# All output tiles of the down projections with the weights stationary, and the last tile's end in two spare banks

## The chip, the cores and the metric

One core of one Trainium2 chip runs the whole kernel in one launch. The metric is the device time of one execution in microseconds; the median of three runs is given. Granted clock 1.00 is TensorE at its 2.4 GHz level.

## What is computed

One layer of an encoder: a half-step SwiGLU feed-forward block, token mixing by two kinds of attention, and a second half-step feed-forward block, each behind a modulated RMS norm. 256 tokens, width 2048, hidden width 5632, all in float32. The change touches the third product of the two feed-forward blocks, the down projection, and its residual:

```python
def swiglu(x, w_gate, w_up, w_down):
    return (jax.nn.silu(x @ w_gate) * (x @ w_up)) @ w_down

f = swiglu(modulate(rms_norm(h, g_ffn1[l]), sh1, sc1), w1_gate[l], w1_up[l], w1_down[l])
h = h + 0.5 * gt1[:, None, :] * f
...
f = swiglu(modulate(rms_norm(h, g_ffn2[l]), sh3, sc3), w2_gate[l], w2_up[l], w2_down[l])
h = h + 0.5 * gt3[:, None, :] * f
```

## The kernel before

**Layout.** The residual h is kept with features on partitions: 16 tiles of 128 features x 256 tokens (`h[d]`, d = 0 to 15). The hidden activation is 44 tiles of 128 hidden features (`hid[f]`), each holding a high part and a low part of 256 tokens side by side. Every weight and activation is split into a high and a low part, and a product is made of three terms: high by high, high by low, low by high.

**The stream of weights.** All weights come through one stream of units (class `Flow`). A unit is 128 x 1024, eight blocks of 128 x 128, and is loaded by SyncE's queue (L77), rounded to its high part by ScalarE three units ahead (L84), and its low part is made by VectorE two units ahead (L91). `step()` advances one unit: it issues these conversions, then the functions that were registered for this unit with `at` or `at_abs` (phase 0, 1, 3), and between them, at a rate set by `pace`, side jobs on VectorE that make the modulation vectors from `w_ada` (L197, with their own loads, L211). `next()` hands out one block (128 x 128), `half()` four blocks side by side (128 x 512). The order of all instructions is the order of the program text; no scheduler reorders it.

**The down stage** is `ffn_down`, called once for each feed-forward block (L626 and L917). It has 16 x 44 blocks, so 88 units, and two forms.

- Three groups (`DG = 3`, L479 to L486) of four output tiles each: the activation is stationary and the weights stream. For each f, and each half t of the tokens, `mm3` (L223) issues three matmuls of 512 columns into the bank of that half (L224 high by high, L225 high by low, L226 low by high). The result has tokens on partitions, so `turn` brings it back: ScalarE copies the two banks to SBUF (L464), in the next unit TensorE makes eight 128 x 128 transposes (L472) into two banks (`pr`), and VectorE folds each tile into h, one operation for a tile (`finish`, L448).
- Four single tiles (L487 to L495): the weight block is stationary and the activation streams. `mm2` (L228) issues one matmul of 512 columns, high weight by high and low activation (L229), and one of 256, low weight by high activation, into the first half of the same bank (L230). `finish` folds both halves of the bank into h (L448, two operations for a tile). For the last tile the folds are issued directly after its last matmul (L497).

In the first stage `finish` also makes the squares of the folded tile (ScalarE) and their running sum (VectorE, L287) for the next norm; `stat.finish` multiplies the sum and the last square by a matrix of ones on TensorE (L300, L302) with matmuls between and after that only keep the engine busy (L296). The next stage's first matmul waits for that norm. In the second stage `finish` stores each tile; the last store ends the kernel.

**What stands before it.** The up projection hands over its last group of hidden tiles (40 to 43) inside the down stage: `hid_soon` combines gate and up on VectorE in the second unit (L385), transposes in the third (L394), rounds on ScalarE in the fourth (L400) and makes the low part on VectorE in the fifth (L407).

Of the kernel before, what the change touches and what calls it, by code (L numbers as in the profile page):

```python
# [9 lines left out]
F32 = mybir.dt.float32  # L10
F32R = mybir.dt.float32r
AF = mybir.ActivationFunctionType
ALU = mybir.AluOpType
AX = mybir.AxisListType

P = 128
S = 256
D = 2048
KT = D // P
DFF = 5632  # L20
FT = DFF // P
# [3 lines left out]
NEG = -1e30  # L25
CW = 1024
SPLIT1 = (3, 8, 16)
DG = 3
SPLIT2 = (4, 10, 16)
PLAN = ((4, 6, 9, 11), (8, 10, 13, 15), (12, 14, 17, 19), (16, 18, 21, 23))  # L30
PLAN_L = ((4, 6, 9, 11), (6, 8, 11, 13), (7, 9, 12, 14), (9, 11, 14, 15))
# [119 lines left out]
def build(tc, a):  # L151
    nc = tc.nc
    with ExitStack() as ctx:
        cp = ctx.enter_context(tc.tile_pool(name="cp", bufs=1))
        wp = ctx.enter_context(tc.tile_pool(name="wp", bufs=2))
        sp = ctx.enter_context(tc.tile_pool(name="sp", bufs=2))
        pb = ctx.enter_context(tc.tile_pool(name="pb", bufs=8, space=bass.MemoryType.PSUM))

        def bank(nm):
            return pb.tile([P, 512], F32, tag="b", name=nm)  # L160
# [4 lines left out]
        fl = Flow(tc, a, wp, srcs)  # L165
# [3 lines left out]
        ident = cp.tile([P, P], F32, name="ident")  # L169
# [6 lines left out]
        h = [h4[k // 4][:, k % 4, :] for k in range(KT)]  # L176
# [28 lines left out]
        def mod(j, k):  # L205
            assert (j, k) in modded, (j, k)
            return acc[:, j, k : k + 1]
# [15 lines left out]
        def mm3(out, lh, ll, rh, rl, first, last, **kw):  # L223
            nc.tensor.matmul(out, lh, rh, start=first, stop=False, **kw)  # L224
            nc.tensor.matmul(out, lh, rl, start=False, stop=False, **kw)  # L225
            nc.tensor.matmul(out, ll, rh, start=False, stop=last, **kw)  # L226

        def mm2(ps, lh, ll, r, first, last):  # L228
            nc.tensor.matmul(ps, lh, r.rearrange("p t s -> p (t s)"), start=first, stop=False)  # L229
            nc.tensor.matmul(ps[:, :S], ll, r[:, 0, :], start=False, stop=last)  # L230
# [115 lines left out]
        part, hid = {}, {}  # L346
# [96 lines left out]
        def ffn_down(jg, stat=None, out=None):  # L443
            def finish(d, u, ps):

                def e0():
                    for p_ in ps:
                        nc.vector.scalar_tensor_tensor(h[d], p_, mod(jg, d), h[d], ALU.mult, ALU.add)  # L448

                fl.at_abs(u, e0)  # L450
                if stat is not None:
                    box = []
                    fl.at_abs(u + 1, lambda: box.append(stat.square(h[d])))
                    fl.at_abs(u + 2, lambda: stat.add(box[0]))
                if out is not None:
                    fl.at_abs(u + 1, lambda: nc.sync.dma_start(out[d], h[d]))

            def turn(G, ps):
                box = {}

                def e0():
                    for t in range(2):
                        box[t] = sp.tile([P, 512], F32, tag="th", bufs=2, name="dt")
                        nc.scalar.copy(box[t], ps[t])  # L464

                def e1():
                    for i in range(2):
                        pt = bank("pr").rearrange("p (f s) -> p f s", f=2)
                        for f in range(2):
                            cs = slice((2 * i + f) * P, (2 * i + f + 1) * P)  # L470
                            for t in range(2):
                                nc.tensor.transpose(pt[:, f, t * P : (t + 1) * P], box[t][:, cs], ident)  # L472
                        for f in range(2):
                            finish(4 * G + 2 * i + f, fl.u + 1 + i, [pt[:, f, :]])

                fl.at(0, e0)
                fl.at(1, e1, 3)

            for G in range(DG):  # L479
                ps = [bank("pd") for t in range(2)]  # L480
                for f in range(FT):
                    whi, wlo = fl.half()
                    for t in range(2):
                        ts_ = slice(t * P, (t + 1) * P)
                        mm3(ps[t], hid[f][:, 0, ts_], hid[f][:, 1, ts_], whi, wlo, f == 0, f == FT - 1)
                turn(G, ps)  # L486
            for d in range(4 * DG, KT):  # L487
                ps = bank("pd")
                for f in range(FT):
                    if d == KT - 1 and f == FT // 2:  # L490
                        fl.pace(0.0)
                    w = fl.next()
                    mm2(ps, *w, hid[f], f == 0, f == FT - 1)
                if d < KT - 1:
                    finish(d, fl.u, [ps[:, :S], ps[:, S:]])  # L495
            for p_ in (ps[:, :S], ps[:, S:]):
                nc.vector.scalar_tensor_tensor(h[d], p_, mod(jg, d), h[d], ALU.mult, ALU.add)  # L497
            if stat is not None:
                stat.add(stat.square(h[d], True))
                stat.finish(hid[0])  # L500
            if out is not None:
                nc.sync.dma_start(out[d], h[d])
# [70 lines left out]
        for c in range(KT):  # L573
            nc.tensor.matmul(
                pm[:, 0:1], zero[c // 8][:, c % 8 * P : (c % 8 + 1) * P], sc2[:, c : c + 1],
                start=c == 0, stop=c == KT - 1)
# [345 lines left out]
def _consts():  # L922
    pos = np.arange(S, dtype=np.float32)
    inv = np.power(500000.0, -np.arange(0, 32, 2, dtype=np.float64) / 32).astype(np.float32)
    ang = (pos[:, None] * inv[None, :]).astype(np.float32).astype(np.float64)
    cs, sn = np.cos(ang).astype(np.float32), np.sin(ang).astype(np.float32)
    rope = np.stack([np.concatenate([cs, cs], 1), np.concatenate([-sn, sn], 1)], 1)
    rope = np.ascontiguousarray(rope.reshape(2, P, 2, 32).transpose(1, 0, 2, 3))
    i = np.arange(S)
    df = i[:, None] - i[None, :]  # L930
    cnt = (np.abs(df) <= 64).astype(int) + (df % 4 == 0) + (df % 16 == 0)
    lnc = np.where(cnt > 0, np.log(np.maximum(cnt, 1)), NEG).astype(np.float32)
    col = i % 64
    start = np.clip(col - 8, 0, 48)
    ok = (col[None, :] >= start[:, None]) & (col[None, :] < start[:, None] + 16)
    nam = np.where(ok, 0.0, NEG).astype(np.float32)
    row = i // 64
    idx = (row[None, :] - row[:, None] + 7) * 31 + np.clip(col[None, :] - col[:, None], -15, 15) + 15

    def lay(m):  # L940
        return np.ascontiguousarray(m.reshape(2, P, S).transpose(1, 0, 2))

    return rope, lay(lnc), lay(nam), idx
# [15 lines left out]
def _arrays(inputs):  # L959
    g = {k: np.asarray(v) for k, v in inputs.items()}  # L960
    rope, lnc, nam, idx = _consts()
    c = np.ascontiguousarray

    def vec(v):
        return np.asarray(v).reshape(-1, P).T

    wq = g["w_qkv"][0].reshape(8, 2, P, 3, 4, 512).transpose(4, 3, 0, 2, 1, 5).reshape(4, 3, 8, P, CW)
    arr = {
        "x": c(g["x"][0].T.reshape(4, 4, P, S).transpose(0, 2, 1, 3)),
        "w_ada": c(g["w_ada"][0].reshape(2, CW, 9 * KT, P).transpose(2, 0, 3, 1)),  # L970
        "vecs": c(np.concatenate([
            vec(g["g_ffn1"][0]), vec(g["g_mix"][0]), vec(g["g_ffn2"][0]),
            vec(g["g_out_na"][0]), vec(g["g_out_dil"][0]), vec(g["c"][0]), vec(g["b_ada"][0])], axis=1)),
        "qkg": c(np.stack([g["qn_na"][0], g["kn_na"][0], g["qn_dil"][0], g["kn_dil"][0]])),
        "rope": rope, "lnc": lnc, "nam": nam,
        "nab": c(g["rpb_na"][0].reshape(8, -1)[:, idx].reshape(8, 2, P, S).transpose(0, 2, 1, 3)),
        "w_qkv": c(np.stack([wq[g_, j, k_] for g_, j, k_ in QKV_ORDER])),
        "w_o": c(g["w_o"][0].reshape(2, 8, P, KT, P).transpose(0, 3, 2, 1, 4).reshape(2 * KT, P, CW)),
    }

    def stream(blocks):
        return c(blocks.reshape(-1, 8, P, P).transpose(0, 2, 1, 3).reshape(-1, P, CW))

    def halves(units):
        return c(units.reshape(-1, 2, P, 512).transpose(0, 2, 1, 3).reshape(-1, P, CW))

    arr["w_zero"] = c(g["w_ada"][0][:, :P].reshape(2, 8, P, P).transpose(0, 2, 1, 3).reshape(2, P, CW))
    for l, cuts in ((1, SPLIT1), (2, SPLIT2)):
        gu = np.stack([g[f"w{l}_gate"][0], g[f"w{l}_up"][0]]).reshape(2, KT, P, FT // 4, 512)
        gu = gu.transpose(3, 0, 1, 2, 4)  # L990
        arr[f"w{l}_s"] = halves(gu[:2, :, : cuts[0]].transpose(2, 0, 1, 3, 4))
        arr[f"w{l}_a"] = halves(gu[2:, :, : cuts[0]])
        arr[f"w{l}_b"] = halves(gu[:, :, cuts[0] : cuts[1]])
        arr[f"w{l}_c"] = halves(gu[:, :, cuts[1] :])
        wd = g[f"w{l}_down"][0]
        arr[f"w{l}_d"] = np.concatenate([
            halves(wd[:, : 512 * DG].reshape(FT, P, DG, 512).transpose(2, 0, 1, 3)),
            stream(wd[:, 512 * DG :].reshape(FT, P, KT - 4 * DG, P).transpose(2, 0, 1, 3))])
    return arr


# [20 lines left out]
```

## Time and profile before

| | us |
|---|---|
| median of three runs | 1912.9 (1912.8 to 1914.55) |
| the profiled execution, its own time | 1914.67 |
| its span, first to last instruction | 1912.9 |
| TensorE matmul busy | 1896.2 |
| VectorE busy | 1526.6 |
| ScalarE busy | 895.5 |
| first down stage, first to last matmul start | 519.4 to 763.4 |
| second down stage, first to last matmul start | 1664.8 to 1908.9 |

The rows further down come from this profiled execution. Times on the left of a row are microseconds from the start of the span. PE is TensorE's matmul side and PEld its loading of stationary operands; DVE is VectorE, ACT is ScalarE, SP is SyncE. A matmul's duration in a row reaches over the start of the next, since they are pipelined; the distance of two starts is what one costs in a stream.

### The profile page before, as it was taken

The page shows a single profiled execution, that of the slowest core. Times are in us where ns is not written, and L with a number is a line of the kernel's source. Part 1 is how long each engine was busy: PE and PEld are TensorE (multiplying, and loading weights), DVE is VectorE, ACT ScalarE, POOL GpSimd, SP SyncE. Part 2 cuts the span into 40 slices and gives each one's busy share as a digit, 9 for nine tenths or more (in the row PEclk, how much of TensorE's full clock was granted, in tenths as well). Part 3 has the DMA queues.
Part 4 walks back from the last instruction along what each step waited for, and adds up shares of the span by engine and source line. Part 5 has one row for each costly group of instructions (what it writes and reads, how often), then busy time and mean ns, then how long its engine had stood idle before and what let it go on. Part 6 is the DMA issues. An engine that isn't in the chain of part 4 may idle for free.

```text
span 1912.9 us, 25124 instructions
## 1 busy us (share of the span) xinstructions
PE 1896.2 (99%) x9105; PEld 1591.3 (83%) x9105; DVE 1526.6 (80%) x2086; ACT 895.5 (47%) x1226; POOL 1.2 (0%) x7
## 2 busy tenths in 40 slices
PE   8999999999999999999999999999999999999999
PEld 6888888888888888888888998888888888888888
DVE  7989988888889888778887988777777888876444
ACT  5654444444444443555555544654443544443342
POOL 0000000000000000000000000000000000000000
PEclk9999999999999999999999999999999999999999
DMA  8998987777799999576766656998888767687664
GB/s 327 368 337 310 308 291 243 247 260 251 245 361 360 350 359 363 186 244 217 243 207 201 209 186 214 310 306 276 271 275 264 220 213 227 220 286 255 200 198 131
DMA packets 140813, 503.85 MB, mean 263 GB/s; under 512 B 15632, under 2 KB 17936, under 8 KB 140688
## 3 DMA queue, kind: packets, MB, share of 16 engines
q1 hardware_dynamic: 140688, 502.25, 78.0%
q8 instruction: 71, 1.16, 0.2%
q14 instruction: 54, 0.44, 0.1%
HBM read 500.09 MB, written 2.10 MB: 263 GB/s over the span
## 4 chain that ended last, share of the span: by engine, by line
PE 94%; DVE 4%; issue 1%; ACT 0%; POOL 0%; POOLq 0%; DVEq 0%
PE pu L224 16%; PE pu L226 16%; PE pu L225 16%; PE pd L225 6%; PE pd L226 6%; PE pd L224 6%; PE pd L229 4%; PE pd L230 2%; PE pqv L224 2%; PE pqk L224 2%; PE pqq L224 2%; PE pqk L225 2%; PE pqk L226 2%; PE pqq L225 2%; PE pqv L226 2%; PE pqq L226 2%
## 5 line engine op out<-in xcount | busy, mean ns | idle before, releaser
L84 ACT CAST hiw<-rw 128x1024 fp32r<-128x1024 f32 x656 | 692.2, 1055 | 954.4 <-PE pu L226 446.1
L91 DVE TENSOR_TENSOR low<-rw,hiw 128x1024 fp32r<-128x1024 f32 x656 | 802.0, 1223 | 336.3 <-issue 126.7
L224 PE MATMUL pu<-hiw,nx 128*128 128x512 f32 x1352 | 527.7, 390 | 0.0
L226 PE MATMUL pu<-hiw,nx 128*128 128x512 f32 x1352 | 526.1, 389 | 0.0
L225 PE MATMUL pu<-low,nx 128*128 128x512 f32 x1352 | 526.1, 389 | 0.0
L226 PEld LDWEIGHTS pu<-hiw,nx 128*128 128x128 f32 x1352 | 253.8, 188 | 53.0
L225 PEld LDWEIGHTS pu<-low,nx 128*128 128x128 f32 x1352 | 253.9, 188 | 51.9
L224 PEld LDWEIGHTS pu<-hiw,nx 128*128 128x128 f32 x1352 | 253.9, 188 | 51.8
L224 PE MATMUL pd<-hiw,hd 128*128 128x512 f32 x528 | 205.9, 390 | 0.0
L226 PE MATMUL pd<-hiw,hd 128*128 128x512 f32 x528 | 205.4, 389 | 0.0
L225 PE MATMUL pd<-low,hd 128*128 128x512 f32 x528 | 205.4, 389 | 0.0
L197 DVE CUSTOM_DVE_ANT_0 ra<-ra,cb,acc 128x1024 f32<-128x1024 f32 x143 | 185.7, 1299 | 0.2
L229 PE MATMUL pd<-hd,hiw 128*128 128x512 f32 x352 | 122.5, 392 | 0.0
L226 PEld LDWEIGHTS pd<-hiw,hd 128*128 128x128 f32 x528 | 99.1, 188 | 20.6
L224 PEld LDWEIGHTS pd<-hiw,hd 128*128 128x128 f32 x528 | 99.1, 188 | 20.4
L225 PEld LDWEIGHTS pd<-low,hd 128*128 128x128 f32 x528 | 99.1, 188 | 20.3
L362 DVE TENSOR_TENSOR pt<-pt,pu 128x512 f32<-128x512 f32 x176 | 112.4, 680 | 0.0
L230 PE MATMUL pd<-hd,low 128*128 128x256 f32 x352 | 98.6, 280 | 0.0
L197 DVE CUSTOM_DVE_ANT_0 ra<-ra,cb,vec 128x1024 f32<-128x1024 f32 x63 | 80.5, 1279 | 0.0
L229 PEld LDWEIGHTS pd<-hd,hiw 128*128 128x128 f32 x352 | 65.8, 187 | 14.4
L224 PE MATMUL pso<-ox,hiw 128*128 128x256 f32 x256 | 73.9, 289 | 0.0
L225 PE MATMUL pso<-ox,hiw 128*128 128x256 f32 x256 | 73.1, 286 | 0.0
(154 smaller groups left out, 2000.5 us busy)
## 6 DMA issues: line engine op xcount, KB each, us to landing
ra<-in_w_ada_dram SPq DMA_DIRECT2D x286, 512.0 KB, 4.9
rw<-in_w_d_dram SPq DMA_DIRECT2D x176, 512.0 KB, 4.6
rw<-in_w_c_dram SPq DMA_DIRECT2D x154, 512.0 KB, 4.3
rw<-in_w_b_dram SPq DMA_DIRECT2D x121, 512.0 KB, 4.8
rw<-in_w_qkv_dram SPq DMA_DIRECT2D x96, 512.0 KB, 4.2
rw<-in_w_a_dram SPq DMA_DIRECT2D x63, 512.0 KB, 4.9
rw<-in_w_o_dram SPq DMA_DIRECT2D x32, 512.0 KB, 3.6
rw<-in_w_s_dram SPq DMA_DIRECT2D x14, 512.0 KB, 4.5
```

Source lines behind the costliest of these rows:

```text
L84: self.nc.scalar.copy(t, self.raw[self.nhi])
L91: self.nc.vector.tensor_tensor(t, self.raw.pop(self.nlo), self.hi[self.nlo].bitcast(F32), ALU.subtract)
L197: nc.vector.tensor_tensor_reduce(out=raw, in0=raw, in1=cb[:, b * CW : (b + 1) * CW], scale=scale, scalar=init, op0=ALU.mult, op1=ALU.add, ...
L224: nc.tensor.matmul(out, lh, rh, start=first, stop=False, **kw)
L225: nc.tensor.matmul(out, lh, rl, start=False, stop=False, **kw)
L226: nc.tensor.matmul(out, ll, rh, start=False, stop=last, **kw)
L229: nc.tensor.matmul(ps, lh, r.rearrange("p t s -> p (t s)"), start=first, stop=False)
L230: nc.tensor.matmul(ps[:, :S], ll, r[:, 0, :], start=False, stop=last)
L362: nc.vector.tensor_tensor(part[G][:, j, t, :], part[G][:, j, t, :], ps[t], ALU.add)
```

## The change

The three groups and their `turn` are gone: all sixteen output tiles take the form with the weight block stationary, in the order d = 0 to 15, and each is folded by `finish` with two operations, in the unit that follows its last block. The array of the down weights is laid out for that, as `stream` blocks throughout; it has as many units as before.

The last tile is cut: its first 36 hidden tiles go to its bank `ps` as the others do, and the last eight blocks (one unit) go to two other banks. First come eight matmuls of 256 columns, high weight by low activation, into `pl`; then the two folds of `ps` and the fold of `pl` are issued; then sixteen matmuls of 256 columns, high and low weight by high activation, into `ph`, and the fold of `ph` follows the last of them.

```diff
-DG = 3
...
-            def turn(G, ps):
...
-            for G in range(DG):
-                ps = [bank("pd") for t in range(2)]
-                for f in range(FT):
-                    whi, wlo = fl.half()
-                    for t in range(2):
-                        ts_ = slice(t * P, (t + 1) * P)
-                        mm3(ps[t], hid[f][:, 0, ts_], hid[f][:, 1, ts_], whi, wlo, f == 0, f == FT - 1)
-                turn(G, ps)
-            for d in range(4 * DG, KT):
+            def fold(d, p_):
+                nc.vector.scalar_tensor_tensor(h[d], p_, mod(jg, d), h[d], ALU.mult, ALU.add)
+
+            for d in range(KT):
                 ps = bank("pd")
-                for f in range(FT):
+                body = FT if d < KT - 1 else FT - 8
+                for f in range(body):
                     if d == KT - 1 and f == FT // 2:
                         fl.pace(0.0)
                     w = fl.next()
-                    mm2(ps, *w, hid[f], f == 0, f == FT - 1)
+                    mm2(ps, *w, hid[f], f == 0, f == body - 1)
                 if d < KT - 1:
                     finish(d, fl.u, [ps[:, :S], ps[:, S:]])
+            ws = [fl.next() for f in range(8)]
             for p_ in (ps[:, :S], ps[:, S:]):
-                nc.vector.scalar_tensor_tensor(h[d], p_, mod(jg, d), h[d], ALU.mult, ALU.add)
+                fl.at(0, lambda p_=p_: fold(d, p_))
+            pl_, ph_ = bank("pl")[:, :S], bank("ph")[:, :S]
+            for f in range(8):
+                nc.tensor.matmul(pl_, ws[f][0], hid[body + f][:, 1, :], start=f == 0, stop=f == 7)
+            fl.run(0)
+            fold(d, pl_)
+            for f in range(8):
+                r = hid[body + f][:, 0, :]
+                nc.tensor.matmul(ph_, ws[f][0], r, start=f == 0, stop=False)
+                nc.tensor.matmul(ph_, ws[f][1], r, start=False, stop=f == 7)
+            fold(d, ph_)
...
         wd = g[f"w{l}_down"][0]
-        arr[f"w{l}_d"] = np.concatenate([
-            halves(wd[:, : 512 * DG].reshape(FT, P, DG, 512).transpose(2, 0, 1, 3)),
-            stream(wd[:, 512 * DG :].reshape(FT, P, KT - 4 * DG, P).transpose(2, 0, 1, 3))])
+        arr[f"w{l}_d"] = stream(wd.reshape(FT, P, KT, P).transpose(2, 0, 1, 3))
```

## Rows read from the trace of the kernel before

**Rows 1.** The page: span, and busy time, share and instructions of each engine.
```profile
span 1912.9 us, 25124 instructions
PE 1896.2 (99%) x9105; PEld 1591.3 (83%) x9105; DVE 1526.6 (80%) x2086; ACT 895.5 (47%) x1226; POOL 1.2 (0%) x7
```

**Rows 2.** The chain that ended last: shares; then start us, us, engine, line.
```profile
PE 94%; DVE 4%; issue 1%; ACT 0%; POOL 0%; POOLq 0%; DVEq 0%
...
1909.18 0.49 DVE h L497
1909.70 0.48 DVE h L497
```

**Rows 3.** Stretches of the down stages: length, busy us by engine, PEclk, DMA share.
```profile
core 0: us, PE busy (x) PEld busy (x) DVE busy (x) ACT busy (x) POOL busy (x), PEclk, DMA share, GB/s
519.37:580.10 60.73, 60.73 (x273) 50.38 (x272) 54.12 (x66) 25.47 (x25) 0.00 (x0) 1.00 0.96 350
...
701.57:763.50 61.93, 61.93 (x361) 54.67 (x360) 54.40 (x75) 26.59 (x31) 0.00 (x0) 1.00 0.96 351
1664.70:1725.30 60.60, 60.60 (x273) 50.30 (x272) 44.22 (x52) 24.19 (x24) 0.00 (x0) 1.00 0.85 283
...
1847.05:1909.20 62.15, 62.09 (x361) 54.55 (x359) 28.75 (x31) 21.02 (x21) 0.00 (x0) 1.00 0.52 158
```

**Rows 4.** Timeline of PE, second stage, wide groups: start us, us, line, tiles.
```profile
1728.31 1.03 PE L472 MATMUL pr<-ident,dt 128*128 128x128 f32 x8
...
1789.04 1.03 PE L472 MATMUL pr<-ident,dt 128*128 128x128 f32 x8
1789.83 0.48 PE L224 MATMUL pd<-hiw,hd 128*128 128x512 f32 x1
1790.14 0.40 PE L225 MATMUL pd<-low,hd 128*128 128x512 f32 x1
1790.38 0.39 PE L226 MATMUL pd<-hiw,hd 128*128 128x512 f32 x1
...
1846.82 0.39 PE L226 MATMUL pd<-hiw,hd 128*128 128x512 f32 x1
```

**Rows 5.** Timeline of PE, second stage, the four narrow tiles.
```profile
1847.05 0.39 PE L229 MATMUL pd<-hd,hiw 128*128 128x512 f32 x1
...
1849.86 1.03 PE L472 MATMUL pr<-ident,dt 128*128 128x128 f32 x8
...
1856.28 0.39 PE L229 MATMUL pd<-hd,hiw 128*128 128x512 f32 x1
...
1908.63 0.39 PE L229 MATMUL pd<-hd,hiw 128*128 128x512 f32 x1
```

**Rows 6.** Timeline of PE in the output projection, 256 columns alone.
```profile
1130.97 0.28 PE L224 MATMUL pso<-ox,hiw 128*128 128x256 f32 x1
...
1162.65 0.28 PE L224 MATMUL pso<-ox,hiw 128*128 128x256 f32 x1
```

**Rows 7.** Timeline at the end of the first down stage; idle time and releaser in brackets.
```profile
763.71 1.01 DVE L497 SCALAR_TENSOR_TENSOR h<-pd,acc,h 128x256 f32<-128x256 f32 x2 [1.49 <-PE pd L230]
...
765.23 0.30 PEld L302 LDWEIGHTS pstat<-sq,ones 128*128 128x128 f32 x2 [0.64 <-DVE sq L273]
```

**Rows 8.** Groups of VectorE in 701.57 to 761: count, busy us, mean ns, idle before.
```profile
L287 DVE TENSOR_TENSOR sqa<-sqa,sq 128x256 f32<-128x256 f32 x7 | 2.9, 419 | 0.2
L448 DVE SCALAR_TENSOR_TENSOR h<-pd,acc,h 128x256 f32<-128x256 f32 x6 | 2.9, 481 | 0.1
L448 DVE SCALAR_TENSOR_TENSOR h<-pr,acc,h 128x256 f32<-128x256 f32 x4 | 1.7, 473 | 0.0
```

**Rows 9.** Timeline at the start of the first down stage: the last hidden group.
```profile
524.82 1.04 PE L394 MATMUL ph<-ident,pt 128*128 128x128 f32 x8
...
531.18 1.23 DVE L91 TENSOR_TENSOR low<-rw,hiw 128x1024 fp32r<-128x1024 f32 x1 [0.23 <-issue]
532.32 1.28 DVE L407 TENSOR_TENSOR hd<-ph,hd 128x512 fp32r<-128x512 f32 x2
533.52 1.33 DVE L197 CUSTOM_DVE_ANT_0 ra<-ra,cb,gin 128x1024 f32<-128x1024 f32 x1
```

More of the change, by code (lines that the diff above doesn't have):

```diff
@@ L456, in finish @@
                     fl.at_abs(u + 1, lambda: nc.sync.dma_start(out[d], h[d]))
-            def turn(G, ps):
-                box = {}
-                def e0():
-                    for t in range(2):
[L463 to L477, printed above, removed]
-            for G in range(DG):
-                ps = [bank("pd") for t in range(2)]
-                for f in range(FT):
-                    whi, wlo = fl.half()
-                    for t in range(2):
-                        ts_ = slice(t * P, (t + 1) * P)
-                        mm3(ps[t], hid[f][:, 0, ts_], hid[f][:, 1, ts_], whi, wlo, f == 0, f == FT - 1)
-                turn(G, ps)
-            for d in range(4 * DG, KT):
+            def fold(d, p_):
+                nc.vector.scalar_tensor_tensor(h[d], p_, mod(jg, d), h[d], ALU.mult, ALU.add)
+            for d in range(KT):
                 ps = bank("pd")
-                for f in range(FT):
+                body = FT if d < KT - 1 else FT - 8
+                for f in range(body):
                     if d == KT - 1 and f == FT // 2:
```

## The prediction

> **What bounds the kernel now.** I read the share of busy time first: TensorE is busy for 1896.2 us of a span of 1912.9 us, no other engine for more than 80% [rows 1]. A busy matmul row overlaps the next one, so that share alone proves nothing; the chain that ended last does, since 94% of it is PE and 4% VectorE [rows 2]. So I went to the two down stages and asked whether TensorE ever waits there. Cut into eight stretches (three wide groups and the four narrow tiles of each stage; four of them are shown, the others read alike), PE is busy throughout, but for the last 0.06 us, and the granted clock is 1.00, the 2.4 GHz level [rows 3]. What sets the time there is therefore the start-to-start step of one matmul to the next, plus whatever stands in TensorE's own program order, and nothing that the other engines do. The steps come from the timeline, by dividing the distance of two starts by the matmuls between them; the durations of the rows (0.39 us) are longer than the steps and aren't used.
>
> Two forms of the same product already run side by side in the kernel, which makes this change unusually easy to price. In the wide form (first three groups, four output tiles each) the activation is stationary and the weights stream, 512 columns in each of six matmuls for one hidden tile f. From 1790.38 to 1846.82 there are 249 steps in 56.44 us, 226.67 ns each [rows 4]. In the narrow form (last four output tiles) the weights are stationary, with one 512- and one 256-column matmul for a block. From 1856.28 to 1908.63 there are 151 blocks in 52.35 us, 346.67 ns each [rows 5].
>
> **The change, part by part (one down stage; there are two).**
>
> *The step.* The wide form spends 6 x 512 columns on four output tiles, so for one tile and one f it is 1.5 matmuls: 1.5 x 226.67 = 340.00 ns. The narrow form streams the same 768 columns, but in two matmuls: 346.67 ns, 6.67 ns more. 12 output tiles x 44 f = 528 blocks move from one form to the other: 528 x 6.67 ns = **+3.52 us**. All of it is on the path.
>
> The rows say why. Matmuls of 256 columns alone (the output projection) step at exactly 120.0 ns: 264 of them from 1130.97 to 1162.65 [rows 6]. So 512 columns cost 226.67 and 256 cost 120.0, which sum to the narrow block's 346.67; 256 columns more cost 106.67, and each matmul carries 13.33 ns that don't depend on its width. The change trades 1.5 of these for 2. The Trainium skill, page "TensorE: Matmul & The Clock Gate", section "Back-to-back issue gap", gives a fixed part of only 2.5 ns on a warm clock. The rows contradict it here by a factor of five; with 2.5 ns the step would cost 0.66 us instead of 3.52 us a stage (an estimate from that page), and no other term of mine hangs on it.
>
> *The turn.* After each wide group the result stands with tokens on partitions: ScalarE copies two banks out, TensorE makes eight 128x128 transposes, VectorE folds four tiles into h. The transposes stand in TensorE's order. From one turn's first transpose to the next it is 1789.04 - 1728.31 = 60.73 us [rows 4]; 264 wide matmuls take 59.84; the turn costs 0.89 us (0.79 of transposes, and the 0.31 us step of the first matmul after them, where 0.23 is usual [rows 4]). Three turns: **-2.67 us**. The two ScalarE copies aren't on the path and bring nothing.
>
> *The first blocks in the new form.* The eight narrow blocks right after the switch take 2.81 us (1847.05 to 1849.86), where eight settled ones take 2.77; after the turn's transposes the pace settles [rows 5]. In the changed kernel the switch lies at the start of the stage, and the next transposes (those of the last hidden group) come two units later, so about 16 blocks run at that pace instead of eight: +0.04 us.
>
> *The tail.* Now both halves of the last tile are folded after the last matmul: two VectorE operations starting 0.52 us apart (1909.18 and 1909.70 [rows 2]), and then the store, or in the first stage the square for the statistics; the same pair takes 1.01 us there [rows 7]. In the changed kernel the last eight blocks go into two other banks: 8 matmuls of 256 columns, then 16. The tile's first 36 blocks are folded under these, the low part under the 16, and one fold is left after the last matmul: -0.52 us. It is gained whole: in the second stage only the store follows; in the first the second half of the statistics' product waits for the square, 0.64 us on the loading side [rows 7]. The price is 24 matmuls of 256 columns for eight blocks, 24 x 120.0 = 2.88 us against 8 x 346.67 = 2.77: +0.11 us. The folds under them need 1.3 us of VectorE, where 2.88 us lie open.
>
> *VectorE's extra folds.* Twelve tiles now have two folds instead of one, and the last has four instead of two: 14 x 0.44 us, off TensorE's path as long as VectorE keeps up. The cover is the proof that already runs: in the stretch of the first stage's narrow tiles VectorE had all its usual work, ten folds and seven sums, 54.4 of 61.9 us busy, and PE didn't wait [rows 3, 8]; the changed stage has eight folds and four sums in as long. The low parts of the weights are made two units ahead, about 5.5 us, and the largest backlog that I find (split of the hidden group, then a fold, in one unit each of 3.3 to 3.7 us against a unit of 2.77) is about 1.1 us.
>
> *The last hidden group.* Hidden tiles 40 to 43 are used in the first group's 21st unit now, and in the sixth after the change. Their transposes run at 524.82, and their last split ends on VectorE by 533.52, in the fifth unit [rows 9]. With the longer units of the changed kernel the fifth begins at 531.4 and the sixth at 534.2; the two splits, 0.64 us each behind a low part of 1.14, then end at 533.2 and 533.9, and their first readers come at 534.2 and 534.9. About 1 us is to spare, so 0; if the split came one unit late it would be up to 1.8 us a stage.
>
> *The rest.* As many units, loads and conversions, in the same order, at the same pace of side jobs; the stores of h start earlier and are spread. The gates for the first tiles are long computed. Nothing of it is priced.
>
> **Sum.** 3.52 - 2.67 + 0.04 - 0.52 + 0.11 = +0.48 us a stage, +1.0 us in all. The profiled execution's span goes from 1912.9 to 1913.9 us, and its own time, 1914.67, to 1915.6; the median of the runs shown is 1912.9, 1.8 below the profiled execution's time, so the forecast for the median is **1913.9 us**. A measurement of this kernel can tell about 0.2%, 3.8 us, from no change.
>
> **The rivals.**
>
> *The unsettled pace stays (slower).* The 351.3 ns of the first eight narrow blocks ended with a turn's transposes; the changed kernel has no turns. If only such a break settles the pace, and those of the hidden group don't, the 688 further blocks of a stage cost 4.6 ns more each: 3.2 us, in all 6.4 + 1.0 = +7.4, **1920.3 us**. It decides the sign from about 300 blocks a stage on. For it: the slow blocks are slow one by one, up to the transposes. Against it: the same eight transposes stand in the third unit of the changed stage, and once settled the pace held for 151 blocks without a break.
>
> *A late split or a VectorE backlog (slightly slower).* The tight place is the sixth unit. A split that is a unit late costs 1.8 us a stage: +4.6, **1917.5 us**. Against it: 1 us to spare and VectorE idle before each low part.
>
> *No fixed part (faster).* If a 256-column matmul cost half a 512-column one, both forms would take 340.0 ns a block. The step would cost nothing: -2.67 + 0.04 - 0.52 = -3.15 a stage, -6.3, **1906.6 us**. Two long runs of rows speak against it [rows 5, 6]. The page named above comes nearest to it: by its 2.5 ns, -4.9 us and 1908.0, an estimate.
>
> *The tail brings nothing.* If the last fold doesn't end earlier (VectorE still at the others), the result is +2.0, 1914.9 us: no change either.
>
> **How the numbers follow.** Forecast and idle tail together 0.86, unsettled pace 0.07, late split 0.04, no fixed part 0.03. Within 0.2%: 0.86; slower: 0.11; faster: 0.03. The terms themselves are known to some tenths; the range adds what medians of three differ by (1.7 us between the runs shown) on both sides and most of the late split above: 1912.0 to 1917.0 us.
>
> **What would show it.** Right: narrow blocks stepping at 346.67 ns through the whole stage; a down stage from its first matmul to its last about 1.0 us longer (3.52 - 2.67 + 0.04 + 0.11), PE without a wait; no transposes besides the hidden group's; one fold after the last matmul, ending 0.5 us nearer to it. Wrong: blocks at 350 ns and more after the first 16; a gap of PE before f = 40 of the first tile; VectorE's low parts arriving late; the last fold waiting for VectorE and not for PE.

## The result, and the profile after

The changed kernel takes 1919.84 us (median of ten runs, 1914.59 to 1926.62) against 1914.46 us for the kernel before (ten runs, 1912.64 to 1915.01): a ratio of 1.0034, 95% interval 1.0025 to 1.0043. The forecast was 1913.9 us and no change within 0.2%. It is slower, by 5.4 us, and its runs spread over 12 us where those of before spread over 2.4. The spread is the first clue: whatever was added isn't the same in every execution.

The profiled execution is one of the quick ones, 1916.61 us, with a span of 1914.8 us. In the two down stages it shows the forecast to 0.05 us, which makes it a trap for a reader who looks at one profile only. The page:

```profile
span 1914.8 us, 26084 instructions
PE 1898.3 (99%) x9601; PEld 1612.8 (84%) x9601; DVE 1538.4 (80%) x2114; ACT 889.5 (46%) x1214; POOL 1.2 (0%) x7
```

It answers to [rows 1]: 496 more matmuls, 2 us more of TensorE, VectorE's share as before. The two down stages, cut from the first matmul of the stage to the first matmul behind it (first stage) or to the end of the last fold (second stage), are the view that carries this case. First the kernel before, then the changed one (columns as in [rows 3]):

```profile
519.37:769.38 250.01, 249.34 (x1198) 209.49 (x1196) 219.60 (x289) 104.45 (x115) 0.00 (x0) 1.00 0.95 351
...
1664.84:1910.18 245.34, 244.30 (x1177) 205.74 (x1175) 137.99 (x147) 93.59 (x93) 0.00 (x0) 1.00 0.69 218
```

```profile
519.72:770.26 250.54, 250.06 (x1446) 220.22 (x1445) 224.97 (x303) 101.21 (x109) 0.00 (x0) 1.00 0.95 350
...
1666.06:1911.87 245.81, 245.29 (x1425) 216.45 (x1423) 144.70 (x161) 90.72 (x87) 0.00 (x0) 1.00 0.67 218
```

The stages are 0.53 and 0.47 us longer; the sum in the prediction was 0.48 for each. The rest of the span's 1.9 us is outside them: in the profiles of this study the first down stage begins between 517.4 and 519.7 us and the stretch between the stages takes from 893.8 to 897.5 us, whatever was changed. So times of single executions differ by some microseconds from this alone, and the stages are compared by their own lengths. The narrow blocks, in the timeline of PE of the same execution: first block of tile 1 and of tile 15, 616 blocks apart, in the first and in the second stage.

```profile
535.96 0.39 PE L228 MATMUL pd<-hd,hiw 128*128 128x512 f32 x1
...
749.51 0.39 PE L228 MATMUL pd<-hd,hiw 128*128 128x512 f32 x1
...
1682.30 0.39 PE L228 MATMUL pd<-hd,hiw 128*128 128x512 f32 x1
...
1895.84 0.39 PE L228 MATMUL pd<-hd,hiw 128*128 128x512 f32 x1
```

213.55 us for 616 blocks, 346.67 ns each, in both stages: the pace of [rows 5]. The end of the second stage, VectorE:

```profile
1908.53 1.00 DVE L458 SCALAR_TENSOR_TENSOR h<-pd,acc,h 128x256 f32<-128x256 f32 x2 [4.27 <-PE pd L229]
1909.63 0.48 DVE L458 SCALAR_TENSOR_TENSOR h<-pl,acc,h 128x256 f32<-128x256 f32 x1
1911.39 0.48 DVE L458 SCALAR_TENSOR_TENSOR h<-ph,acc,h 128x256 f32<-128x256 f32 x1 [1.27 <-PE ph L481]
```

Three of the four folds run under the 24 last matmuls, which start from 1908.32 to 1911.07 us, and one is left behind them, where [rows 2] had two. So the page of this execution has no 5 us. They had to be sought in another execution.

### The profile page after: what moved, and what is told of

It reads as the page before. It is cut to its first block, busy times and chain, and to the rows that moved or that the text cites. A ratio compares the mean times of both kernels' runs of the same rounds, so it can differ in the third digit from the quotient of the medians.

```text
span 1914.8 us, 26084 instructions
## 1 busy us (share of the span) xinstructions
PE 1898.3 (99%) x9601; PEld 1612.8 (84%) x9601; DVE 1538.4 (80%) x2114; ACT 889.5 (46%) x1214; POOL 1.2 (0%) x7
## 4 chain that ended last, share of the span: by engine, by line
PE 93%; DVE 6%; issue 1%; ACT 0%; POOL 0%; POOLq 0%; DVEq 0%
PE pd L228 17%; PE pu L223 16%; PE pu L225 16%; PE pu L224 16%; PE pd L229 9%; DVE low L90 2%; PE pqv L223 2%; PE pqk L223 2%; PE pqq L223 2%; PE pqk L224 2%; PE pqk L225 2%; PE pqq L224 2%; PE pqv L225 2%; PE pqq L225 2%; PE pqv L224 2%; PE ph L393 1%
## 5 line engine op out<-in xcount | busy, mean ns | idle before, releaser
L228 PE MATMUL pd<-hd,hiw 128*128 128x512 f32 x1392 | 483.1, 391 | 0.0
L229 PE MATMUL pd<-hd,low 128*128 128x256 f32 x1392 | 389.8, 280 | 0.0
L228 PEld LDWEIGHTS pd<-hd,hiw 128*128 128x128 f32 x1392 | 260.3, 187 | 57.2
L229 PEld LDWEIGHTS pd<-hd,low 128*128 128x128 f32 x1392 | 263.1, 189 | 0.1
L225 PE MATMUL pso<-ox,low 128*128 128x256 f32 x256 | 73.0, 285 | 0.0
L196 DVE CUSTOM_DVE_ANT_0 ra<-ra,cb,gin 128x1024 f32<-128x1024 f32 x48 | 64.2, 1338 | 0.0
L223 PE MATMUL pqk<-hiw,nx 128*128 128x512 f32 x128 | 51.2, 400 | 0.0
L223 PE MATMUL pqv<-hiw,nx 128*128 128x512 f32 x128 | 50.5, 395 | 0.5 <-ACT nx L317 0.5
L223 PE MATMUL pqq<-hiw,nx 128*128 128x512 f32 x128 | 50.9, 398 | 0.0
```

The lines of the kernel that those rows point to most:

```text
L196: nc.vector.tensor_tensor_reduce(out=raw, in0=raw, in1=cb[:, b * CW : (b + 1) * CW], scale=scale, scalar=init, op0=ALU.mult, op1=ALU.add, ...
```

## The experiments

Two words first. **Short pace** and **long pace** are the two steps of a narrow block (one 512- and one 256-column matmul) that the profiles of this order of matmuls show, 346.67 and 353.33 ns on average. Times against before compare medians with those of the kernel before, run beside it on the same chip. The expectations call the short pace fast and the long one slow. The code is abridged: `...` and the comments stand for what isn't shown.

**e1, the changed kernel again**, for a second profile. No edit.

> The changed kernel once more, for the spread of its executions and for another profile. The forecast's theory (one step of 346.67 ns a block, nothing else) gives a span of 1913.9 us in every execution; the ten timed ones had spans from 1912.8 to 1924.8, so something comes on top that varies from one execution to the next. Unsettled pace: some executions keep 351 ns a block over long stretches, up to 6.4 us more, and the profile of a slow one has blocks at 350 ns and over after the first 16. Supply: in some executions TensorE waits, for a weight part, a load or its own instructions, and the profile of a slow one has gaps of 0.5 us and more in a down stage.

Measured: 1921.84 us (1921.75 to 1923.77) against 1912.72, ratio 1.0049 (1.0036 to 1.0063). The profile has a span of 1921.8 us; the stages first, then the first blocks of tile 1 and tile 15 in each stage, as above.

```profile
519.26:774.32 255.06, 254.58 (x1446) 220.84 (x1444) 225.96 (x303) 101.07 (x109) 0.00 (x0) 1.00 0.93 343
...
1668.54:1918.88 250.34, 249.82 (x1425) 217.07 (x1423) 144.65 (x161) 90.41 (x87) 0.00 (x0) 1.00 0.63 213
```

```profile
535.67 0.40 PE L228 MATMUL pd<-hd,hiw 128*128 128x512 f32 x1
...
753.32 0.40 PE L228 MATMUL pd<-hd,hiw 128*128 128x512 f32 x1
...
1684.95 0.40 PE L228 MATMUL pd<-hd,hiw 128*128 128x512 f32 x1
...
1902.60 0.40 PE L228 MATMUL pd<-hd,hiw 128*128 128x512 f32 x1
```

217.65 us for the same 616 blocks: 353.33 ns each, without a wait of PE inside (its busy time fills the stages but for the same 0.5 us as above, the norm behind the first and the last fold of the second), at a granted clock of 1.00. The long pace holds from the transposes of the last hidden group to the end of the stage, 680 blocks x 6.67 ns = 4.53 us, and the stages are 4.52 and 4.53 us longer than in the first profile. The two stages together are 9.05 us longer, the span 7.0: outside the stages this execution was 2.0 us shorter than the first (894.22 us between them against 895.80), so the long pace is the whole excess. The supply theory falls: nothing waited.

Three blocks of this profile show where the time goes, and one block of the first profile (its last row begins the next block):

```profile
599.62 0.40 PE L228 MATMUL pd<-hd,hiw 128*128 128x512 f32 x1
599.85 0.28 PE L229 MATMUL pd<-hd,low 128*128 128x256 f32 x1
599.97 0.40 PE L228 MATMUL pd<-hd,hiw 128*128 128x512 f32 x1
600.21 0.28 PE L229 MATMUL pd<-hd,low 128*128 128x256 f32 x1
600.33 0.40 PE L228 MATMUL pd<-hd,hiw 128*128 128x512 f32 x1
600.56 0.28 PE L229 MATMUL pd<-hd,low 128*128 128x256 f32 x1
600.68 0.40 PE L228 MATMUL pd<-hd,hiw 128*128 128x512 f32 x1
```

```profile
599.75 0.39 PE L228 MATMUL pd<-hd,hiw 128*128 128x512 f32 x1
599.98 0.28 PE L229 MATMUL pd<-hd,low 128*128 128x256 f32 x1
600.09 0.39 PE L228 MATMUL pd<-hd,hiw 128*128 128x512 f32 x1
```

At the long pace the blocks aren't alike: they take 350, 361 and 349 ns in turn, 1.06 us for three. Over the stages of these two profiles the mean step from a 512-column matmul to the 256-column one behind it is 236.67 ns at the long pace and 230.00 at the short, and the step back is 116.67 in both: all the 6.67 ns come behind the matmul of 512 columns.

**e2 and e3, one stage changed.** The three wide groups stay in the other stage.

```diff
-DG = 3
+DGS = (0, 3)          # e3: (3, 0)
+TAIL = (True, False)  # e3: (False, True): the cut tail
...
```

> Only the first down stage is changed (all narrow, cut tail); the second is as before. Forecast's sum: +0.5 us over before. Supply theory: the first stage loads at 0.96 of the DMA engines and VectorE is 90% busy there, so nearly the whole excess of the changed kernel (some +5 us) and its spread are here. Unsettled pace: half of the excess, about +2.5 to +3.2 us, since both stages have the same matmuls.

> Only the second down stage is changed; the first is as before. Forecast's sum: +0.5 us over before. Supply theory: within 1 us of before, since the second stage loads at 0.5 to 0.86 of the DMA engines and VectorE is 46 to 73% busy. Unsettled pace: half of the excess, +2.5 to +3.2 us.

Measured: 1918.45 us for e2 (ratio 1.0034, 1.0021 to 1.0046) and 1920.02 us for e3 (1.0038, 1.0025 to 1.0050) against 1912.72. In their profiles the changed stage has the long pace and the unchanged one doesn't: 255.07 and 245.34 us for the stages of e2, 250.00 and 250.34 for those of e3, so each stage brings its 5.0 us by itself. e3's median is 2 us above that, but its profile isn't: its span is 4.96 us longer than that of the profile before, all of it in the second stage, and outside the stages the two agree to 0.1 us (895.44 us between the stages against 895.46). The 2 us are what that execution of before (1914.67 us) itself lies above the median here. The load on the DMA engines (0.95 in the first stage, 0.67 in the second) makes no difference.

**e4, the tail alone.** Three wide groups in both stages, and only the last tile's end cut.

```diff
-DG = 3
+DGS = (3, 3)
+TAIL = (True, True)
...
```

> The kernel before with the cut tail in both stages and nothing else (three wide groups each). Forecast's terms: -0.52 + 0.11 = -0.41 us a stage, -0.8 us in all. If the tail brings nothing or starves something, 0 or more.

Measured: 1911.79 us (1910.65 to 1914.47, eleven runs) against 1912.72, ratio 0.9997 (0.9988 to 1.0005): not to be told from no change by its time. The stages of its profile tell it:

```profile
519.05:768.68 249.63, 249.17 (x1206) 209.94 (x1204) 220.37 (x291) 104.43 (x115) 0.00 (x0) 1.00 0.95 351
...
1662.52:1907.43 244.91, 244.39 (x1185) 206.18 (x1183) 138.84 (x149) 93.62 (x93) 0.00 (x0) 1.00 0.67 218
```

0.38 and 0.43 us shorter than before, where 0.41 was forecast for each. It is the one part of the change that was run by itself and shortened a stage.

**e5, breaks.** Ahead of tiles 1 to 14 in both stages, a short piece of TensorE work into a spare bank, six kinds in turn.

```diff
...
+                if kind in "AB":   # 8 transposes, 1 transpose
+                    nc.tensor.transpose(idle[:, ...], ident, ident)
+                else:              # 2 x 512, 1 x 256, 3 x 256, 4 x 128 columns
+                    nc.tensor.matmul(idle[:, :w_], hid[0][:, 0, :P], r_, start=True, stop=True)
```

> The changed kernel with a short foreign piece of TensorE work ahead of each output tile d = 1 to 14, in both stages: eight transposes, one transpose, two matmuls of 512 columns, one of 256, three of 256 or four of 128 columns, in turn (their results are not used). Theory that the pace is drawn anew at each break of the alternation and kept until the next: within one execution some tiles step at 346.67 and some at 353.33 ns, and it changes only at a break. Rival, that the pace belongs to the execution (or the chip): all tiles of an execution have one pace, whatever stands between them. Second rival, that only transposes (or a pause) settle it: the tiles behind the transposes differ from those behind plain matmuls.

Measured: 1930.8 us (one run, the breaks' own time included). Each tile behind a break has one pace throughout (twelve blocks at a time, without the first six, take 346.6 to 346.7 or 353.2 to 353.3 ns a block), and it is always one of the two:

| ahead of the tile | tiles at the short pace |
|---|---|
| two matmuls of 512 columns | 4 of 4 |
| one of 256 | 5 of 5 |
| three of 256 | 4 of 5 |
| eight transposes | 2 of 5 |
| one transpose | 2 of 5 |
| four of 128 | 0 of 4 |

So the pace belongs neither to the execution nor to the chip: both occur within one stage, and it changes at breaks alone. Nor does it belong to a place in the weights, since the same tiles had the one pace in the first profile and the other in e1. The table doesn't say what pace stood ahead of a break. By the same trace, the four tiles ahead of the breaks of four 128-column matmuls were short and those behind them long; one transpose left the pace as it was in five of five; four of the five single matmuls of 256 columns stood behind a tile that was short already, and one ended a long one. (The next expectations speak of four tiles behind one matmul of 256 columns; there were five.)

**e6, grouped, and e7, pairs.** The same matmuls in another order: four of 512 columns and then four of 256 for four blocks (e6); high, low, low, high for two blocks (e7).

```diff
-                    mm2(ps, *w, hid[f], f == 0, f == body - 1)
...
+                    for f in fs: nc.tensor.matmul(ps, w[f - f0][0], ...)          # 512 columns
+                    for f in fs: nc.tensor.matmul(ps[:, :S], w[f - f0][1], ...)   # 256 columns
```

> The changed kernel with the same matmuls in another order: of four blocks the four of 512 columns first, then the four of 256. If the extra 6.67 ns of a block comes from alternating 512 and 256 columns matmul by matmul, runs of one width have none of it: 4 x 226.67 + 4 x 120.0 = 1386.7 ns for four blocks, 346.67 each, in every execution, or with one such loss for four blocks at most 348.3; the kernel is at the forecast, +1.0 us over before (at most +3.4), with as little spread as before. If the loss belongs to the stationary weights as such: +8 us as the changed kernel.

> The changed kernel with the order high, low, low, high over two blocks: half as many changes from 512 to 256 columns. If the loss is one for each change of width in this alternation, the slow pace is 350.0 ns a block (half of 6.67), about +1 to +5.7 us over before; if the loss needs the strict alternation, +1.0 us; if it belongs to the stationary weights as such, +8 us as the changed kernel.

Measured against 1913.09: e6 1921.46 us (1919.88 to 1922.22), ratio 1.0039 (1.0026 to 1.0052); e7 1916.71 us (1915.01 to 1920.13), ratio 1.0017 (1.0008 to 1.0026). The grouped order, which I took for the cure, isn't one:

```profile
599.73 1.09 PE L469 MATMUL pd<-hd,hiw 128*128 128x512 f32 x4
600.66 0.64 PE L472 MATMUL pd<-hd,low 128*128 128x256 f32 x4
601.14 1.09 PE L469 MATMUL pd<-hd,hiw 128*128 128x512 f32 x4
602.07 0.63 PE L472 MATMUL pd<-hd,low 128*128 128x256 f32 x4
602.54 1.09 PE L469 MATMUL pd<-hd,hiw 128*128 128x512 f32 x4
```

Eight blocks in 2.81 us are 351 ns each. Four matmuls of 512 columns take 0.93 us to the next start, where 4 x 226.67 are 0.91, while those of 256 take 0.47 to 0.48: the loss sits in the matmuls of 512 columns. It isn't at the change of width: from 530 to 755 us of this profile the step from one of 512 to the next is 233.6 ns on average, and from the last of them to the first of 256 it is 228.3. The profile of e7, its quickest execution, steps at 348.3 ns a block. Fewer changes of width don't give the sum of the single steps back, so the loss isn't simply one for each change.

**e8, the cut tail with the grouped order in the four narrow tiles**, three wide groups kept. The edits of e4 and e6 together.

> The kernel before (three wide groups a stage) with the cut tail and the grouped order in its four narrow tiles. Sum: -0.8 us from the tail; the grouped order takes away the slow pace in the narrow tiles where they have it (at most 176 x 6.67 ns = 1.2 us a stage), and otherwise nothing: -0.8 to -3 us against before.

Measured: 1914.99 us (1913.20 to 1915.65) against 1913.09, ratio 1.0004 (0.9995 to 1.0013): the grouped order gives away what the tail brings. The stages of its profile are 0.3 and 0.2 us longer than before, where the tail alone made them 0.4 shorter.

**e9, e10, e11, one break in each stage**, ahead of tile 1; and **e12**, the changed kernel beside them.

```diff
+                if d == 1:
...
+                    for i in range(n):   # e9: 1 x 256 columns, e10: 2 x 512, e11: 4 x 128
+                        nc.tensor.matmul(idle, hid[0][:, 0, :P], r_, start=True, stop=True)
```

> The changed kernel with one more matmul of 256 columns, into a spare bank, ahead of the second output tile of each down stage; nothing else. In the run with breaks all tiles behind such a matmul stepped at 346.67 ns (four of four). Theory that the break sets the pace for all that follows: tiles 1 to 15 step at 346.67 ns in both stages and in every execution; forecast's +1.0 us, 0.25 for the two matmuls and up to 0.4 for a slow first tile: +1.2 to +1.7 us over before, with no execution more than 3 us above the median. Rival, that the pace of the executions is set by something else (the chip, the loads): a spread as wide as that of the changed kernel beside it.

> The same with two matmuls of 512 columns in place of the one of 256 (four of four tiles at 346.67 ns in the run with breaks). Same theory: +1.7 to +2.4 us over before (two times 0.45 us for the matmuls), and no wide spread. Rival: a spread as wide as that of the changed kernel.

> The same with four matmuls of 128 columns (four of four tiles at 353.33 ns in the run with breaks). Theory: tiles 1 to 15 step at 353.33 ns in both stages and in every execution: 652 blocks x 6.67 ns = 4.35 us a stage, with the forecast's 1.0 and some 0.5 for the matmuls +10 us over before, though it issues about as much work as the other two. Rival: no difference from them.

> The changed kernel beside them on the same chip. Theory: each stage is fast or slow as its only break, the transposes of the last hidden group, leaves it, so executions lie near +1, +5.7 or +10.4 us over before (and within 2.4 us of these, which before spreads by itself), and its profile has one pace, 346.67 or 353.33 ns, from the 17th block on in each stage.

Measured against 1912.86:

| | median, range (us) | ratio, 95% interval | pace from tile 1 on in the profile, first and second stage |
|---|---|---|---|
| e9, one of 256 | 1915.28 (1914.61 to 1917.13, 11 runs) | 1.0011 (1.0002 to 1.0019) | short, short |
| e10, two of 512 | 1918.21 (1918.17 to 1925.86, 6 runs) | 1.0036 (1.0023 to 1.0049) | long, long |
| e11, four of 128 | 1921.32 (1915.73 to 1921.99, 5 runs) | 1.0032 (1.0020 to 1.0044) | short, short |
| e12, changed kernel | 1920.39 (1917.26 to 1921.94, 5 runs) | 1.0035 (1.0022 to 1.0048) | long, short |

e9 first. The blocks of its first tile have the long pace; then comes one more matmul, and the 652 blocks behind it step at 346.67 ns (533.95 to 759.64, 651 steps):

```profile
533.71 0.28 PE L229 MATMUL pd<-hd,low 128*128 128x256 f32 x1
533.83 0.28 PE L467 MATMUL idle<-hd 128*128 128x256 f32 x1
533.95 0.40 PE L228 MATMUL pd<-hd,hiw 128*128 128x512 f32 x1
...
759.64 0.39 PE L228 MATMUL pd<-hd,hiw 128*128 128x512 f32 x1
```

All its eleven runs lie within 2.5 us, where those of before spread over 3.4 beside them, so it isn't likely that any has the 4.5 us of a stage at the long pace. The median is 2.4 us above before, 0.7 more than expected; the stages of the profile are 0.8 longer each. Two matmuls of 0.12 us whose results nobody uses take back two thirds of what the change loses on this chip, by the medians (7.5 us in e12). e10 and e11 came out against their expectations: the kinds that had been 4 of 4 and 0 of 4 in one execution were long, long and short, short in these profiles, and their runs spread like those of the changed kernel. So these kinds don't set the pace. Whether they draw it is less clear: in both stages of e11 the tile ahead of the break was long, and in e5 it was short, so four matmuls of 128 columns changed the pace in six of six cases. A break that turns the pace over would fit these profiles as well as a draw; no run was made to tell the two apart. For two of 512 columns it doesn't hold: behind a long tile they left the pace short three times in e5 and long twice in e10.

e12 has one stage of each, 5.06 and 0.47 us longer than before:

```profile
519.05:774.12 255.07, 254.59 (x1446) 220.74 (x1445) 225.89 (x303) 101.04 (x109) 0.00 (x0) 1.00 0.94 344
...
1669.81:1915.62 245.81, 245.29 (x1425) 216.45 (x1423) 144.68 (x161) 90.75 (x87) 0.00 (x0) 1.00 0.66 217
```

**e13 and e14, the same matmul elsewhere.** e13: ahead of the first and of the 17th block of each stage; e14: ahead of each of the tiles 1 to 14.

```diff
+                    if d == 0 and f in (0, 16):      # e13;  e14: if 0 < d < KT - 1, ahead of the tile
+                        nc.tensor.matmul(bank("idle")[:, :S], hid[0][:, 0, :P], hid[0][:, 0, :], start=True, stop=True)
```

> The changed kernel with one matmul of 256 columns ahead of the first block of each down stage and one ahead of the 17th (right behind the last hidden group's transposes). If one such matmul sets the fast pace wherever it stands: all 704 blocks of both stages at 346.67 ns, about +1.3 us over before (1.0, less 0.2 for the first blocks, and 0.5 for four matmuls), spread as before. If it only helped by chance: stages at 353.33 ns in some executions, up to +10 us.

> The changed kernel with one matmul of 256 columns ahead of each of the tiles 1 to 14, in both stages: 28 draws. If it sets the pace: all 28 tiles behind one at 346.67 ns. If every break is a draw like those of the transposes (four of sixteen stages fast so far): some 10 to 20 of 28 slow. The time is that of before + 1.0 + 28 x 0.12 = +4.4 us if all are fast.

Measured: e14 1916.27 us (one run; before 1913.08), and 28 of 28 tiles at the short pace. e13 1916.28 us (1914.70 to 1918.29, eleven runs), ratio 1.0013 (1.0004 to 1.0022): behind the transposes the matmul worked in both stages; behind the wide stream it did nothing, and the 16 blocks there stayed at 353.3 ns:

```profile
519.17 0.39 PE L225 MATMUL pu<-hiw,nx 128*128 128x512 f32 x1
519.40 0.28 PE L468 MATMUL idle<-hd 128*128 128x256 f32 x1
519.51 0.40 PE L228 MATMUL pd<-hd,hiw 128*128 128x512 f32 x1
519.74 0.28 PE L229 MATMUL pd<-hd,low 128*128 128x256 f32 x1
519.86 0.40 PE L228 MATMUL pd<-hd,hiw 128*128 128x512 f32 x1
```

There it stands behind a matmul of 512 columns, as any low block does, so the alternation just begins one matmul earlier. In e9 and e14 it makes two of 256 columns in a row, and in e13's other place it follows transposes. The 28 tiles of e14 count for less than they seem: 27 of them stood behind a tile that was short already, and one behind a long one.

The expected +1.3 us of e13 wasn't met: its median is 3.2 us above before. The stages of its profile account for 1.5 us, and the stretch between them took 897.46 us, 2.0 more than in the profile before.

## Why the prediction was wrong

- **The step, the turn, the tail: right.** In the profile with both stages at the short pace the stages grew by 0.53 and 0.47 us for a sum of 0.48, and the tail alone (e4) gave -0.38 and -0.43 for -0.41. The reason given for the step held less well: 226.67 and 120.0 ns do sum to the short pace, but inside the block the steps are 230.0 and 116.67, and the same matmuls took 351 and 348.3 ns a block in other orders (e6, e7), so a block isn't the sum of two steps that each width carries with it. The fixed part of 2.5 ns that the Trainium skill gives for a single matmul ("TensorE: Matmul & The Clock Gate", section "Back-to-back issue gap") would have made the stages shorter. The traces don't agree: no stage of sixteen narrow tiles was shorter than the 250.01 and 245.34 us of before in any profile.
- **"The first blocks in the new form": the step that failed.** It was put at +0.04 us a stage, and where the long pace stayed it was 4.53. I read the eight longer blocks behind the switch as a passing state that any transposes end, because the rows of before showed it ended by the turn's transposes in both stages. Two cases were taken for a rule. In the profiles of this study the turn's transposes ended it in six of six stretches (before, e2 to e4), but those of the last hidden group, to which I passed the task on, in only five of eighteen; and in e5 eight transposes did so in two of the four places where the pace ahead was long.
- **The rival was the mechanism, at the wrong price and with the wrong chance.** "The unsettled pace stays" was priced as all or nothing, 4.6 ns a block, +7.4 us, with 0.07. Each stage has its own pace, so one stage at the long pace is a case of its own: 1.0 + 4.53 = +5.5 us, where the medians lie 5.4 apart; both make +10.1, where e1 measured 9.1. Which paces the ten timed runs had is not on record, so this goes by the sizes alone. The 4.6 ns came from a mean over the first eight blocks, which took in the quicker first ones; the settled difference is 6.67. That the rival's 1920.3 us lies 0.5 us from the measured median is luck: it stands for +7.4 us over the 1912.9 us of before, and what was measured is +5.4 over 1914.46. And it couldn't decide the sign from 300 blocks on, as the prediction has it, since the sum was above zero without it; 300 blocks a stage are what it takes to leave the 0.2%.
- **VectorE's folds, the last hidden group, the late split: right, and without cost.** PE waits for nothing in any changed stage, though VectorE has 14 more folds.
- **Why the kernel before is steady** follows from the same runs: its wide groups step at 226.67 ns in every profile, and only 176 blocks a stage could have the long pace, 1.2 us; in the six stretches seen they had it for eight blocks.

What stays open: what in TensorE makes a narrow block 6.67 ns longer, why the hidden group's transposes mostly leave the long pace and the turn's never did, and why one more matmul of 256 columns ends it. One added matmul of another width wasn't run, so it isn't shown that the 256 columns are what counts. The runs show when it happens and what ended it, not the cause inside the engine. As for a better kernel, e4 is the best that was run, 0.9 us under before by its medians, which its interval doesn't separate from no change.

## What to carry to other kernels

A pace read from a short stretch of the old kernel may be one of several that the same instructions can have; before it is multiplied by hundreds of blocks, look at how it began and whether what set it is still there after the change. When the runs of a kernel spread more than those of its parent, profile it more than once, since one profile shows one of the cases. And a step that is longer by a fixed few nanoseconds, with no wait in the profile, can be tested by one foreign instruction in the stream.

## What the runs showed of the hardware that I had not expected

- The same alternation of matmuls with 512 and 256 columns, at a granted clock of 1.00, runs at 346.67 or at 353.33 ns a pair on average, one or the other, and holds it for as long as 680 pairs (240 us); in these profiles the pace changes only where something else stands between.
- One added matmul of 256 columns behind another of 256 columns ended the long pace in four of four cases seen in the profiles (one tile of e5, two stages of e9, one tile of e14) and left the short one in 31 of 31; three of them in a row left it in four of five. Eight transposes ended the long pace in six of six turns, but in seven of 22 cases elsewhere (five of eighteen stages, two of four tiles of e5).
- Long streams of one width have only one step: 226.7 to 227.1 ns for 512 columns and 120.0 for 256 in every profile. Mixing the two costs more than their sum in some orders: 351 ns a block in groups of four, 348.3 in pairs.
